# Rotating an 8192 x 8192 matrix: macro tiles of 2048 columns, with four load buffers of half the size and four store buffers

## Chip, cores and metric

One core of one Trainium2 chip. The metric is the device time of one launch in microseconds (us), the median of several runs. The kernel before takes 1275.95 us (three runs, 1274.87 to 1276.43).

## The reference

```python
x = np.random.randn(8192, 8192).astype(np.float32)   # 268.4 MB
np.rot90(x, 1)                                        # out[i, j] = x[j, 8191 - i]
```

Every element is read once and written once: 536.9 MB of traffic and no arithmetic.

## The kernel before

The matrix is handled in macro tiles of 1024 rows by 4096 columns. Loads bring 128 rows each (2 MB, 16 KB a row). VectorE copies each load into chunks of 128 x 512 with the order of columns reversed in each block of 128. TensorE transposes 128 x 128 blocks into PSUM, ScalarE copies PSUM into a store buffer, and ScalarE's queue issues a 2 MB store.

```python
R = 1024; RT = R // P; W = 4096; CH = 512; G = 4; PW = 2
...
    a_pool = ctx.enter_context(tc.tile_pool(name="a_pool", bufs=2))     # 2 x 16 KB a partition
    r_pool = ctx.enter_context(tc.tile_pool(name="r_pool", bufs=68))    # chunks, 2 KB each
    o_pool = ctx.enter_context(tc.tile_pool(name="o_pool", bufs=2))     # 2 x 16 KB
...
        for t0 in range(0, RT, q):
            if loads < 2:
                a = o_pool.tile([P, W], dt, tag="o")     # the first two loads borrow store buffers
            else:
                a = a_pool.tile([P, W], dt, tag="a")
            loads += 1
            ...                                          # nc.sync.dma_start(out=a, in_=x[...])
            ...                                          # VectorE: a -> chunks
        for g0 in range(0, C // P, G):
            ...                                          # 32 transposes, 2 ScalarE copies
            nc.scalar.dma_start(out=dst, in_=o[...])
```

A macro tile has 64 chunks, and a store tile needs chunks of all its eight loads. So the first store can go only when a whole macro tile is in. The last macro tile is cut into 2048, 1024 and 1024 columns. A function run at the end of the build, `whole_reads`, rewrites the read side of a transfer so that a row of a store buffer is read as one run of 16 KB, although it is written to HBM in four runs of 4 KB.

## Time and profile before

| what | value | from |
|---|---|---|
| span of the profiled run | 1274.2 us | page |
| PE, VectorE, ScalarE busy | 56%, 28%, 37% | page |
| DMA rate, 120 to 1100 us | 428 GB/s | table by stretches |
| load, store: issue to landing | 16.6 us, 15.9 us | page |
| median packet of 16 KB | 611 ns load, 615 ns store | packet records |

Engines at half load and DMA at 99% mean that only the DMA columns matter. One more view of the kernel before: VectorE's timeline from 20 to 50 us. Each line is the copy of one 2 MB load; the columns are start, busy time, and in brackets how long VectorE was idle before and for whom. (In such lines DVE is VectorE, ACT ScalarE, PE and PEld are TensorE's matmuls and weight loads, and L111 is a line of the kernel.)

```profile
22.76 2.77 DVE L111 COPY ar<-a 128x512 f32<-128x512 f32 x8 [2.12 <-DMA a<-in_x_dram]
29.79 2.77 DVE L111 COPY ar<-a 128x512 f32<-128x512 f32 x8 [4.25 <-DMA a<-in_x_dram]
35.39 2.77 DVE L111 COPY ar<-a 128x512 f32<-128x512 f32 x8 [2.83 <-DMA a<-in_x_dram]
42.46 2.77 DVE L111 COPY ar<-a 128x512 f32<-128x512 f32 x8 [4.29 <-DMA a<-in_x_dram]
```

The copies of the first four loads start 4.9 us apart, the fourth at 22.76 us. The next three come 5.6 to 7.1 us apart.

### The profile page before, as it was taken

The page shows a single profiled execution, that of the slowest core. Times are in us where ns is not written, and L with a number is a line of the kernel's source. Part 1 is how long each engine was busy: PE and PEld are TensorE (multiplying, and loading weights), DVE is VectorE, ACT ScalarE, POOL GpSimd, SP SyncE. Part 2 cuts the span into 40 slices and gives each one's busy share as a digit, 9 for nine tenths or more (in the row PEclk, how much of TensorE's full clock was granted, in tenths as well). Part 3 has the DMA queues.
Part 4 walks back from the last instruction along what each step waited for, and adds up shares of the span by engine and source line. Part 5 has one row for each costly group of instructions (what it writes and reads, how often), then busy time and mean ns, then how long its engine had stood idle before and what let it go on. Part 6 is the DMA issues. An engine that isn't in the chain of part 4 may idle for free.

```text
span 1274.2 us, 10388 instructions
## 1 busy us (share of the span) xinstructions
PE 719.2 (56%) x4096; PEld 685.5 (54%) x4096; DVE 355.2 (28%) x1024; ACT 466.9 (37%) x257; POOL 0.7 (0%) x6
## 2 busy tenths in 40 slices
PE   1455556556655665556546565565565665665564
PEld 0355556555554655556546555565555554665564
DVE  4422232223222322232223222322232222321210
ACT  0233343334334333343334333433343333434444
POOL 0000000000000000000000000000000000000000
PEclk9968686877777677776886867768777778678878
DMA  9999999999999999999999999999999999999998
GB/s 375 366 427 427 427 428 431 429 428 428 430 428 430 428 427 429 429 429 429 427 427 427 429 427 428 427 427 429 428 427 426 424 423 429 427 425 422 420 408 338
DMA packets 39105, 537.55 MB, mean 422 GB/s; under 512 B 4112, under 2 KB 4112, under 8 KB 6160
## 3 DMA queue, kind: packets, MB, share of 16 engines
q1 hardware_dynamic: 20480, 268.44, 49.8%
q10 hardware_dynamic: 18576, 268.44, 49.8%
q8 instruction: 32, 0.52, 0.2%
q14 instruction: 17, 0.14, 0.0%
HBM read 268.44 MB, written 268.44 MB: 421 GB/s over the span
## 4 chain that ended last, share of the span: by engine, by line
DMA 84%; DVE 12%; issue 2%; ACT 1%; PE 0%; DVEq 0%; SPq 0%; ACTq 0%
DMA a<-in_x_dram 81%; DVE ar L111 12%; DMA out_dram<-ot 3%; ACT ot L133 1%; PE ps L128 0%; DVEq L111 0%; SPq L100 0%; ACTq L133 0%; ACTq L141 0%
## 5 line engine op out<-in xcount | busy, mean ns | idle before, releaser
L128 PE MATMUL ps<-ident,ar 128*128 128x128 f32 x4096 | 719.2, 358 | 543.8 <-ACT ot L133 500.2
L128 PEld LDWEIGHTS ps<-ident,ar 128*128 128x128 f32 x4096 | 685.5, 192 | 577.3 <-ACT ot L133 530.5
L133 ACT COPY ot<-ps 128x2048 f32<-128x2048 f32 x256 | 465.6, 1870 | 789.3 <-DMA out_dram<-ot 733.5
L111 DVE COPY ar<-a 128x512 f32<-128x512 f32 x1024 | 355.2, 421 | 894.4 <-DMA a<-in_x_dram 894.4
L133 ACT ACT_TABLE_LOAD x1 | 1.3, 1283 | 10.9 <-DVE ar L111 10.9
masks.py:199 POOL TENSOR_SCALAR_AFFINE_SELECT ident<-ident 128x128 f32<-128x128 f32 x1 | 0.3, 292 | 0.1
masks.py:197 POOL MEMSET ident<- 128x128 f32 x1 | 0.2, 204 | 0.3 <-POOLq L160 0.3
L160 POOL MEMSET const-bfloat16-1.0<- 128x1 bf16 x1 | 0.1, 102 | 0.0
L160 POOL MEMSET const-uint8-127<- 128x1 uint8 x1 | 0.1, 102 | 0.0
L160 POOL MEMSET const-float32-0.0<- 128x1 f32 x1 | 0.1, 99 | 0.2 <-issue 0.2
L160 POOL MEMSET const-float32-1.0<- 128x1 f32 x1 | 0.1, 99 | 0.0
## 6 DMA issues: line engine op xcount, KB each, us to landing
a<-in_x_dram SPq DMA_DIRECT2D x128, 2048.0 KB, 16.6
out_dram<-ot ACTq DMA_DIRECT2D x127, 2048.0 KB, 15.9
out_dram<-ot ACTq DMA_DIRECT2D x2, 1024.0 KB, 5.7
```

The source lines that it names most:

```text
L111: nc.vector.tensor_copy(out=ar[:], in_=a[:, u, j * CH : (j + 1) * CH].rearrange("r (b m) -> r b m", m=P)[:, :, ::-1],)
L128: nc.tensor.transpose(ps[:, PW - 1 - w, t * P : (t + 1) * P], chunks[t, g * P // CH][:, g % (CH // P), :], ident,)
L133: nc.scalar.copy(o[:, G - PW - h : G - h, :], ps[:])
L160: nc = _bacc.Bacc("TRN2", target_bir_lowering=False, num_devices=1)
```

## The change

The intent: smaller macro tiles fill sooner, and four buffers on each side keep more transfers in flight. The sum of memory stays at about 200 KB a partition.

```diff
-W = 4096
+W = 2048
...
-        widths = [W] * (M // W)
+        widths = [2048] * 4
...
-            widths[-1:] = [2048, 1024, 1024]
+            widths = [2048, 2048, 2048, 1024, 1024]
...
-    a_pool = ctx.enter_context(tc.tile_pool(name="a_pool", bufs=2))
-    r_pool = ctx.enter_context(tc.tile_pool(name="r_pool", bufs=68))
-    o_pool = ctx.enter_context(tc.tile_pool(name="o_pool", bufs=2))
+    a_pool = ctx.enter_context(tc.tile_pool(name="a_pool", bufs=4))
+    r_pool = ctx.enter_context(tc.tile_pool(name="r_pool", bufs=52))
+    o_pool = ctx.enter_context(tc.tile_pool(name="o_pool", bufs=4))
...
-            if loads < 2:
-                a = o_pool.tile([P, W], dt, tag="o")
+            if loads < 4:
+                a = o_pool.tile([P, G * R], dt, tag="o")
```

Load rows become 8 KB and loads 1 MB; stores stay 2 MB with 16 KB read runs.

## The prediction

> **What bounds the kernel now.** I read the page's busy table and slices first, then the longest waits, then the DMA view and the table by stretches for the steady part, and last the timeline of the start. On the page:
>
> ```profile
> PE 719.2 (56%) x4096; PEld 685.5 (54%) x4096; DVE 355.2 (28%) x1024; ACT 466.9 (37%) x257; POOL 0.7 (0%) x6
> DMA  9999999999999999999999999999999999999998
> GB/s 375 366 427 427 427 428 431 429 428 428 430 428 430 428 427 429 429 429 429 427 427 427 429 427 428 427 427 429 428 427 426 424 423 429 427 425 422 420 408 338
> q1 hardware_dynamic: 20480, 268.44, 49.8%
> q10 hardware_dynamic: 18576, 268.44, 49.8%
> ```
>
> No compute engine is busy over 56%. The 16 DMA engines are: queue 1 (loads) and queue 10 (stores) together take 99.6% of their time, and the rate is flat at 427 to 430 GB/s except in the first two slices and the last two or three. Each queue moves 268.44 MB, which the problem fixes. 536.9 MB at 428.5 GB/s is 1253 us; the other 21 us of the 1274.2 us span lie in the two ends. The waits agree:
>
> ```profile
> DVE ar L111 <- DMA a<-in_x_dram: 894.4, 128, 15.4
> ACT ot L133 <- DMA out_dram<-ot: 733.5, 122, 11.4
> PEld ps L128 <- ACT ot L133: 530.5, 127, 11.5
> ```
>
> VectorE waits for loads, ScalarE for stores to free its buffer, TensorE for ScalarE: everybody waits for DMA in the end. Nowhere in the steady part does VectorE wait for TensorE. The DMA view from 120 to 1100 us:
>
> ```profile
> DMA packets 28797, 419.33 MB, mean 428 GB/s; under 512 B 3197, under 2 KB 3197, under 8 KB 3197
> q10 hardware_dynamic: 14379, 209.39, 50.4%
> q1 hardware_dynamic: 14379, 209.41, 50.1%
> ```
>
> Both queues carry equal packets there, and 100 loads and 100 stores in 980 us make one 2 MB load plus one 2 MB store every 9.8 us. Only the price of a byte on the DMA engines, and idle DMA at the ends, can move the time. By stretches (the last two columns are DMA busy share and GB/s):
>
> ```profile
> 4.00:20.00 16.00, 2.04 (x6) 0.87 (x6) 7.68 (x23) 1.28 (x1) 0.00 (x0) 1.00 1.00 430
> 20.00:50.00 30.00, 4.37 (x16) 2.78 (x17) 13.85 (x41) 0.00 (x0) 0.00 (x0) 1.00 0.92 349
> 50.00:80.00 30.00, 16.80 (x108) 15.65 (x106) 8.99 (x26) 11.04 (x7) 0.00 (x0) 0.77 1.00 412
> 120.00:1100.00 980.00, 572.89 (x3200) 549.16 (x3200) 277.50 (x800) 362.73 (x200) 0.00 (x0) 0.75 1.01 428
> 1140.00:1187.00 47.00, 29.08 (x192) 27.53 (x192) 11.10 (x32) 21.82 (x12) 0.00 (x0) 0.82 1.01 423
> 1240.00:1274.00 34.00, 16.59 (x128) 15.52 (x128) 2.77 (x8) 16.62 (x10) 0.00 (x0) 0.82 0.83 347
> ```
>
> From 20 to 50 us the rate falls to 349. The timeline tells why: four loads go out at the start (two into store buffers, two into load buffers); the fifth needs a load buffer and is issued only at 20.67 us, after the third has landed and VectorE has spent 2.77 us copying it out. From then on two load buffers alternate, loads land about every 6.3 us instead of every 4.9, and no store can go before 54 us.
>
> **What the Trainium skill says.** "DMA: Bandwidth & Descriptors", section "Where 436 GB/s comes from", puts the ceiling of the 16 engines at 435 GB/s. The trace agrees: 428 to 430. So no layout of buffers can gain much over the steady part. The same page, "Why small descriptors are slow (HBM only)", gives a fixed overhead per packet. The packet records of this trace agree in form: the median packet of 4096, 8192 and 16384 bytes took 159, 309 and 611 ns, a straight line with 8 to 9 ns fixed. (8 KB and 4 KB packets occur in the last tiles, which the kernel before already narrows.) The same page, "Queues, rings and completion order", says that an engine takes turns between queues packet by packet; the equal counts above agree. After the change a load packet is half a store packet, so while both queues hold work stores should get two thirds of the bytes. "SBUF — State Buffer", "The DMA setup-cost knee", charges about 2 us fixed to each transfer and so favours large ones; the 430 GB/s with four loads in flight shows that this is hidden when several overlap, so I charge nothing for 1 MB loads.
>
> **The change, part by part.** Compute is the same: 4096 transposes, 1024 VectorE copies of 421 ns, 256 ScalarE copies of 1870 ns, 129 stores. Loads are 256 of 1 MB instead of 128 of 2 MB, and their rows 8 KB instead of 16 KB.
>
> 1. Load packets. In the kernel before, 120 loads x 128 rows = 15360 packets are of 16 KB. Each becomes two of 309 ns, 618 against 611: +7 ns. 15360 x 7 / 16 engines = **+6.7 us**, all on the path, as DMA never rests.
> 2. Completion packets. Each DMA leaves one 4-byte packet of 9 ns on each engine. 128 more DMAs: **+1.2 us**. SyncE's issue of 0.33 us each is hidden.
> 3. Start. The first eight loads have buffers (four store, four load) and make a whole macro tile, so they run without any wait. Then a load buffer is away for VectorE's 4 x 0.35 = 1.4 us, the issue and some 2 us of start, while three other loads need 3 x 2.45 us: no gap. What the stretches lose now: 30 x (1 - 349/428) = 5.5 us, and 30 x (1 - 412/428) = 1.1 us. I give back **-6 us** of these 6.6. The 2 us to the first byte stays. That the first store goes at some 30 us instead of 54 is worth nothing by itself: bytes are bytes.
> 4. End. From 1240 us DMA is 0.83 busy, 34 x 0.17 = 6 us lost. Four store buffers should remove the waits for a store there (4 to 5 us before a ScalarE copy), but the last macro tile is the same 1024 columns: after its last load, copies, 64 transposes and the last store must follow. With store packets favoured 2:1 or 4:1 over loads, the store backlog will be gone by then, so this chain stands more exposed: I estimate 1.4 + some 7 + 4.9 + 5 us and two latencies, about 20 us, with 9.8 us of data. **+2 us**, uncertain by 4.
> 5. Bursts. Now load and store march 1:1 and both queues always hold two transfers. Afterwards four stores go at two thirds of the rate (7.3 us each, 29 us), then the store queue empties until the next macro tile is complete, some 10 us. DMA still has loads to do: 52 chunk buffers hold one macro tile (32) plus five loads, and four load buffers more. But switches cost something: in 1140 to 1187 us, where 8 KB loads meet 16 KB stores and the store queue runs dry, the rate is 423 against 428, 1.2% less. Load packets (40% of the bytes) explain half of it; the other half went with single packets of 500 to 1000 ns where a queue restarts. At 0.3% of 1250 us: **+3 us**, perhaps 0 and perhaps 12.
>
> Sum: +6.7 + 1.2 - 6 + 2 + 3 = +7 us; 1276 + 7 = 1283, and I say 1282.
>
> **Rivals.** (a) Deeper buffers win: if the lockstep of two transfers per queue were hiding a loss, four would show it. Against it: busy share 1.01 and 428 of 435 GB/s from 120 to 1100 us; at most the 12 us lost at the ends could come back, 1264. (b) The bursts make TensorE the bound: a store tile needs 32 transposes, 5.1 to 6.4 us in the timeline, so stores cannot be fed faster than about 2.1 MB / 5.8 us = 360 GB/s; that matters only if loads stop meanwhile, that is if chunk buffers run out. With 20 spare chunks against 4 before, I think not; if it did happen each macro tile could lose a microsecond or two, 32 to 64 us, 1310 to 1340. (c) The half-size rows read worse from HBM than the medians say, as the 423 stretch might mean if all its loss were the packets': then 1.5% on the whole, about 1295. (d) The restart losses vanish because the other queue is deep: 1277 to 1279.
>
> **Range and chances.** (d) and the sum with modest bursts make the middle, 1277 to 1288; (c) is the upper end; a perfect end and start the lower. 1270 to 1296 should hold it 8 times in 10. Within 2% is 1250 to 1301: gains have no room to reach 1250, as the steady part alone takes 1253; only (b), or (c) with bursts, passes 1301.
>
> **What would show it.** Queue 1 should have 37888 packets (31744 of 8 KB, 2048 of 4 KB, 4096 completions) and queue 10 the same 18576. The second slice should rise from 366 to 420 or more; the middle should read 422 to 427 instead of 428, with uneven slices; the 8 KB packet should have a median of 309 ns. Load time to landing should swing between about 10 us and 20 us where it is now a constant 16.6. VectorE's waits should still be for loads and ScalarE's more for TensorE than for stores. I am wrong if VectorE waits for TensorE in the middle (chunks), if the DMA share there falls under 0.98, or if the mean 8 KB packet exceeds 320 ns.

## The result and the profile after

1285.72 us (median of four runs, 1282.6 to 1289.65) against 1276.11 us: ratio 1.0079, 95% interval 1.005 to 1.0107. A ratio is the mean time of one kernel's runs over that of the other's in the same rounds, so it is not quite the ratio of the medians. The interval is clear of 1: it is a little slower, by about 10 us.

The page of the changed kernel, the lines that answer to those of before:

```profile
PE 611.6 (48%) x4096; PEld 572.9 (45%) x4096; DVE 366.8 (29%) x1024; ACT 467.8 (36%) x257; POOL 0.7 (0%) x6
GB/s 393 424 425 427 424 428 427 425 429 427 423 423 425 424 419 419 419 419 428 424 423 414 427 427 424 414 423 423 423 416 419 425 420 408 426 424 422 405 423 307
q1 hardware_dynamic: 37888, 268.45, 50.2%
q10 hardware_dynamic: 18576, 268.44, 49.6%
```

The second slice rose from 366 to 424: the start is repaired. The middle fell from a flat 428 to an uneven 408 to 429. The loads' queue holds exactly the 37888 packets foreseen. Its time is 50.2% of 1284.2 us, some 645 us, where it was 49.8% of 1274.2, some 635; the packet records say 645.2 against 634.9, and 636.9 against 634.5 for stores.

The waits, longest first (total us, times, longest):

```profile
DVE ar L111 <- DMA a<-in_x_dram: 860.5, 244, 10.5
PEld ps L128 <- ACT ot L133: 636.7, 128, 11.3
...
ACT ot L133 <- DMA a<-in_x_dram: 602.7, 80, 11.2
ACT ot L133 <- PE ps L128: 165.9, 48, 19.9
...
ACT ot L133 <- DMA out_dram<-ot: 10.3, 2, 5.4
```

ScalarE hardly waits for stores any more (733.5 us before, 10.3 now). But it waits for *loads*, 602.7 us. No copy of ScalarE reads a load buffer, so this needs an explanation; the timeline gives it (ACTq is the issue of a store by ScalarE's queue):

```profile
304.87 1.86 ACT L133 COPY ot<-ps 128x2048 f32<-128x2048 f32 x1
...
316.10 0.55 ACTq L141 DMA_DIRECT2D out_dram<-ot  x1
316.15 1.43 DVE L111 COPY ar<-a 128x512 f32<-128x512 f32 x4 [4.73 <-DMA a<-in_x_dram]
```

The store tile is complete at 306.73 us and its store is issued at 316.10, in the same moment as VectorE starts on a fresh load. The trace has eight completion semaphores for all DMAs, and the build hands them out in turn. The issue times read as if a DMA has to wait until the last one on its semaphore has landed. In the kernel before loads and stores alternate, and eight back in turn is always one of the same kind, which landed 23 us or more earlier. In the changed kernel there are two loads to a store, and eight back from a store in that turn is a load (five back in the order of issue). The records show it: of 98 stores issued from 120 to 1100 us, 97 were issued within 0.3 us of the landing of the load that last had their semaphore. So stores in flight averaged 1.27 and were never more than two. Counting from ScalarE's first copy into a store buffer to the landing, at most three of the four buffers were held at once, three of them for 25% of that time.

By stretches (after the window and its length, busy us and number of instructions of PE, PEld, VectorE, ScalarE and GpSimd, then TensorE's granted clock; the last two columns are DMA busy share and GB/s):

```profile
4.00:20.00 16.00, 4.09 (x12) 1.73 (x12) 8.59 (x24) 1.28 (x1) 0.00 (x0) 1.00 1.01 426
20.00:50.00 30.00, 18.55 (x122) 16.25 (x122) 11.45 (x32) 14.65 (x8) 0.00 (x0) 0.88 1.01 420
50.00:80.00 30.00, 17.48 (x122) 16.20 (x122) 8.60 (x24) 11.02 (x6) 0.00 (x0) 0.72 1.01 425
120.00:1100.00 980.00, 469.39 (x3151) 444.11 (x3152) 282.26 (x788) 359.07 (x198) 0.00 (x0) 0.75 1.01 422
1240.00:1284.00 44.00, 20.21 (x147) 18.11 (x145) 4.30 (x12) 18.38 (x10) 0.00 (x0) 0.77 0.81 341
```

From 20 to 50 us 420 GB/s instead of 349; in the middle 422 instead of 428, with DMA fully busy. So in the middle it is the packets that take longer, not idle engines. The medians are as before (309 ns for 8 KB, 614 for stores). Two measures from the packet records serve below, both for 120 to 1100 us:

- *Slow packets*: what packets took beyond the median of their size and queue, summed and divided by the 16 engines. It was 3.5 us before and is 11.5 us now.
- *Dry*: a queue is dry while fewer than two of the 16 engines work on it. The store queue was dry 0.5% of the time before and is dry 21% now.

Of the 11.5 us, 10.0 come from packets that start while neither queue is dry, and they gather about the restarts of the store queue (52 of them after more than 0.5 us dry). Of the 6.2 us of load packets, 2.3 fall in the first 2 us after a restart, with 6% of the packets; of the 5.3 us of store packets, 4.8 fall 2 to 6 us after one.

### The profile page after: what moved, and what is told of

The parts are those of the page before. It is cut to its first block, busy times and chain, and to the rows that moved or that the text cites. A ratio compares the mean times of both kernels' runs of the same rounds, so it can differ in the third digit from the quotient of the medians.

```text
span 1284.2 us, 10957 instructions
## 1 busy us (share of the span) xinstructions
PE 611.6 (48%) x4096; PEld 572.9 (45%) x4096; DVE 366.8 (29%) x1024; ACT 467.8 (36%) x257; POOL 0.7 (0%) x6
## 3 DMA queue, kind: packets, MB, share of 16 engines
q1 hardware_dynamic: 37888, 268.45, 50.2%
## 4 chain that ended last, share of the span: by engine, by line
DMA 89%; DVE 6%; PE 1%; issue 1%; ACT 1%; DVEq 0%; SPq 0%; ACTq 0%
DMA a<-in_x_dram 89%; DVE ar L111 6%; PE ps L128 1%; ACT ot L133 1%; DVEq L111 0%; SPq L100 0%; ACTq L141 0%; DVEq L174 0%; ACTq L133 0%
## 5 line engine op out<-in xcount | busy, mean ns | idle before, releaser
L128 PE MATMUL ps<-ident,ar 128*128 128x128 f32 x4096 | 611.6, 320 | 661.9 <-ACT ot L133 605.8
L128 PEld LDWEIGHTS ps<-ident,ar 128*128 128x128 f32 x4096 | 572.9, 168 | 700.4 <-ACT ot L133 636.7
L133 ACT COPY ot<-ps 128x2048 f32<-128x2048 f32 x256 | 466.5, 1870 | 800.9 <-DMA a<-in_x_dram 602.7
L111 DVE COPY ar<-a 128x512 f32<-128x512 f32 x1024 | 366.8, 421 | 898.7 <-DMA a<-in_x_dram 860.5
```

The costliest lines, as they stand in the source:

```text
L111: nc.vector.tensor_copy(out=ar[:], in_=a[:, u, j * CH : (j + 1) * CH].rearrange("r (b m) -> r b m", m=P)[:, :, ::-1],)
L128: nc.tensor.transpose(ps[:, PW - 1 - w, t * P : (t + 1) * P], chunks[t, g * P // CH][:, g % (CH // P), :], ident,)
L133: nc.scalar.copy(o[:, G - PW - h : G - h, :], ps[:])
```

## The experiments

Three theories. **P**: the price of more packets is the whole loss. **A**: engines take turns between the queues packet by packet, so 16 KB store packets beside 8 KB load packets drain the store queue faster than loads can refill it, and running dry and restarting costs. **T**: the semaphore shared with a load starves the store queue.

### Load packets of 8 KB in the kernel before (e1_half_rows)

```diff
-        for t0 in range(0, RT, q):
+        Cs = min(C, 2048); q = W // Cs
+        for t0, c in [(t, s) for t in range(0, RT, q) for s in range(0, C, Cs)]:
...              # in_=x[r0 + t0*P : r0 + (t0+q)*P, c0 + c : c0 + c + Cs]
```

> The kernel before with one thing changed: each 2 MB load takes two row blocks of 2048 columns instead of one of 4096, so its packets are 8 KB; macro tiles, number of DMAs and buffers stay (at most four transfers in flight). Theory P (the price of a packet: 2 x 309 - 611 = 7 ns on each of 15360): +6.7 us, about 1283, few slow packets in the middle. Theory A (unequal packets alone let the store queue run dry and restart, which costs slow packets): like the changed kernel in the middle, about 422 to 424 GB/s, 1287 to 1292. If the tie of completion semaphores is needed for the slow packets, there are none here, as P says.

Measured: 1321.38 us, ratio 1.0347 (1.0331 to 1.0363). P is far off, and even A's own number was too small. The DMA view from 120 to 1100 us, one rate per fortieth:

```profile
GB/s 363 427 425 396 405 427 427 375 428 427 379 429 426 399 405 427 426 372 426 427 374 427 426 396 408 426 426 368 427 422 354 432 423 395 408 426 426 381 430 428
```

It swings between full rate and 354 to 408. The store queue is dry 26% of the time, and the slow packets (23.7 us) sit mostly where loads run alone: 22 us of them start while the store queue is dry, and DMA is only 0.94 busy then. There two load buffers are in the same need as at the start, when 349 GB/s was reached. Stores finish early, then wait for the next macro tile, and loads alone with two buffers don't fill DMA. So this run adds the shortage of load buffers to the effect of unequal packets; the changed kernel, with four, has less of it. No store here follows closely on a load that had its semaphore, so T has no part in it.

### The same, with store packets of 8 KB too (e8_equal_8k)

```diff
-                    ap = [ap[0], [1, 1], [1, ap[1][1] * ap[2][1]]]
+                    ap = [ap[0], [2048, ap[1][1] * ap[2][1] // 2048], [1, 2048]]
```

> The run with half rows (8 KB load packets, 1321 us) with one more thing changed: the stores' reads are cut in two as well, so store packets are 8 KB too; nothing else. Packets are equal again, at 8 KB. Theory A (unequal packets drain the store queue): although every transfer now has smaller packets, it gets much faster, back to the kernel before plus the price of the packets, (7 ns x 15360 + 3 ns x 16384) / 16 = 10 us: 1284 to 1288, store queue dry under 3%. If small load packets themselves were slow with 2 MB loads, it stays at 1315 or above.

Measured: 1282.32 us, ratio 1.0042 (1.0029 to 1.0055). The same view:

```profile
GB/s 427 427 426 428 427 427 427 427 427 427 427 427 427 427 428 427 426 427 426 427 424 426 427 425 427 426 425 428 424 427 427 424 425 427 427 424 416 423 425 425
```

Making the stores' packets *smaller* wins 39 us and makes them equal; the store queue is dry 3.7% of the time. (Loads of 16 KB with stores of 8 KB were not run: that equal packets are better, and not just store packets no larger than the loads', is tried in this direction alone.) This run is also the price of small packets by itself, all other things as in the kernel before: +0.42%, 5.4 us for both directions, where the medians had said 10. In the records the packets of the two queues took 11.0 us more (1280.4 against 1269.4), while the span grew by 6.0: packet times overlap a little (busy share 1.01), and a sum of them is not time on the clock.

### The changed kernel with equal packets, in two ways

**Stores of 8 KB reads (e11_equal_reads)**, the same edit of `whole_reads`, nothing else.

> The changed kernel with the stores' reads cut in two, so that store packets are 8 KB as the load packets are; still 2 MB stores, four buffers, and every store still shares its completion semaphore with an earlier load. Theory A (unequal packets): store queue no longer dry, slow packets of some 9 us go, 3 us more for packets: 1278 to 1281. Theory T (the semaphore shared with a load starves the store queue): dry about 20% as it is, 1286 to 1290.

Measured: 1278.01 us, ratio 1.0009 (0.9997 to 1.0022). Its middle stretch, to be compared with the 422 GB/s of the changed kernel:

```profile
120.00:1100.00 980.00, 565.43 (x3168) 541.85 (x3168) 283.32 (x791) 358.91 (x199) 0.00 (x0) 0.75 1.01 425
```

Of 99 store issues from 120 to 1100 us, 98 still follow within 0.3 us on the landing of a load, as T wants it, but the store queue is dry 4% instead of 21% and the slow packets halve (5.7 us). At the end, DMA stands idle for 5.7 of the last 44 us, as in the kernel before (5.7; 8.2 in the changed kernel). T by itself starves nothing; the unequal packets carry the loss. Whether they would cost as much with four load buffers and no tie was not tested.

**Store tiles of half the size (e2_small_stores)**

```diff
-G = 4
+G = 2
-    ... name="o_pool", bufs=4
+    ... name="o_pool", bufs=8
```

> The changed kernel with store tiles of 8 KB (two blocks instead of four, eight buffers), so load and store packets are equal again, both 8 KB. Theory P: store packets double, 2 x 312 - 615 = 9 ns on 16384 at most, +9 us and 128 more completions +1.2: 1293 to 1297. Theory A (unequal packets make the store queue run dry): the store queue is almost never dry, the slow packets of some 8 us go, which pays for most of the packets: 1284 to 1289, dry share of the store queue under 5% where it is 21% now.

Measured: 1279.63 us, ratio 1.002 (1.0009 to 1.0032); better than A's range. Loads and stores alternate one to one here, so a store follows a store on its semaphore: up to four 1 MB stores are in flight, dry share 0.3%, slow packets 2.2 us. On the whole that is no better than e11 with its tie to loads, so removing the tie gains nothing in sum once packets are equal. By stretches it is less plain: the middle reads 426 GB/s against 425, but 1190 to 1240 us reads 372 against 407, and there are 128 more completions to pay for.

### Two store buffers (e3_two_stores)

```diff
-    ... name="o_pool", bufs=4
+    ... name="o_pool", bufs=2
-            if loads < 4:
+            if loads < 2:
```

> The changed kernel with two store buffers instead of four (first two loads in store buffers, not four): at most six transfers in flight, fewer than the eight completion semaphores. Theory T (stores wait for the load that last used their semaphore, which starves the store queue): stores wait for stores or TensorE again, the store queue is dry less than 21% of the time, slow packets about halve: 1280 to 1283. Theory A (unequal packets do it): dry share and time as they are, 1284 to 1288. If four store buffers were of real use, it gets slower, over 1289.

Measured: 1283.25 us, ratio 1.0052 (1.0037 to 1.0068); the interval overlaps that of the changed kernel. The premise of this test was wrong: I had thought that six transfers in flight would free the semaphores. They are handed out in turn whatever is free, and 98 of 99 stores still followed within 0.3 us on a load. Dry share 22%, slow packets 10.4 us: as in the changed kernel. What it does show is that taking away the third and fourth store buffer loses nothing.

### A spacer between the DMAs (e6_no_tie)

```diff
+            if loads % 2 == 0:
+                one = d_pool.tile([1, 1], dt, tag="one")
+                nc.sync.dma_start(out=one, in_=x[r0 : r0 + 1, c0 : c0 + 1])
```

> The changed kernel with one 4-byte load more after every second load, which no one reads; completion semaphores are handed out in turn, and with four transfers a round instead of three each store follows a store on its semaphore, not a load. Packets stay unequal. Theory T: slow packets halve, 1279 to 1282. Theory A: with unequal packets the store queue still runs dry about a fifth of the time, 1283 to 1289; stores in flight rise above the 1.27 of now only in bursts.

Measured: 1329.25 us, ratio 1.0417. A failed instrument. The spacers did not stay in their places: they gathered, and on SyncE's queue they stood behind loads that waited. From 120 to 1100 us 77 of 94 stores still shared their semaphore with a load and 16 with a spacer. From 150 to 330 us stores then waited for spacers:

```profile
ACT ot L138 <- DMA one<-in_x_dram: 132.3, 14, 9.9
```

It says nothing on A or T. The rate was 310 to 330 GB/s where stores waited for spacers.

### Two load buffers (e7_two_loads)

```diff
-    ... name="a_pool", bufs=4
+    ... name="a_pool", bufs=2
```

> The changed kernel with two 8 KB load buffers instead of four. If the four load buffers are what keeps DMA full while the store queue is dry, two of 1 MB cannot (a buffer is away 1.4 us for the copy, 0.4 for the issue and some 2 for the start, against 2.45 us for the other load): the load-only stretches fall to about 350 GB/s and the time goes to 1310 to 1330 as with half rows. If load buffers don't matter, 1284 to 1288.

Measured: 1396.47 us, ratio 1.0936. The direction is right, the size is not. Two things come together. Already with loads alone, 4 to 20 us, it reaches less than the 426 of four buffers:

```profile
4.00:20.00 16.00, 4.10 (x12) 1.73 (x12) 8.60 (x24) 1.28 (x1) 0.00 (x0) 1.00 0.94 387
```

And the load to which a store is tied is now the one issued just two before it (91 of 91), so a store starts when the loads end and the two take turns: both queues are dry over 40% of the time. With four load buffers the tie is five back, and e11 shows it harmless. So the change needs its four load buffers; how the 111 us against the changed kernel divide between the two effects stays open. The records say where the time went: DMA was still 0.99 busy from 120 to 1100 us, but store packets took 64.5 us beyond their median, 48.6 of them while the load queue was dry. Neither effect says why.

### Mending the start of the kernel before

The changed kernel showed that the start can be mended. Can the kernel before have that without small packets?

**First macro tile in narrow tiles (e5_start)**: `widths[:1] = [1024, 1024, 2048]`.

> The kernel before with the first 4096-column macro tile split into 1024, 1024 and 2048 columns (2 MB loads as before): the first tile is complete after two loads, so stores start near 17 us and fill the DMA while two load buffers alternate. If the loss at the start (349 GB/s from 20 to 50 us) is what the changed kernel won back, this wins it without small packets: 1270 to 1272, ratio 0.995 to 0.997. If not, 1276.

Measured: 1278.98 us, ratio 1.0017 (1.0003 to 1.0031). The stretch from 20 to 50 us rises to 404 GB/s, but narrow tiles have small load packets beside 16 KB stores, 50 to 80 us reads 399, and 2.6 us of slow packets follow from 120 to 169 us (0.1 before).

**First macro tile in two of half height (e9_half_height)**, so packets stay 16 KB:

```diff
+            if r0 == 0 and c0 == 0:
+                yield 0, 0, C, R // 2
+                yield R // 2, 0, C, R // 2
...              # G, PW and the store's rows follow from the height
```

> The kernel before with its first macro tile cut in height instead of width: twice 512 rows of 4096 columns, so load packets stay 16 KB and equal to the store packets. Complete after four loads, which all have buffers, so stores start near 30 us instead of 54 and fill the DMA while the two load buffers alternate. If unequal packets are what took back the gain of the start made of narrow tiles (1279), this one keeps it: 1272 to 1274. If an early start of stores is worth nothing, 1276 to 1277.

Measured: 1276.92 us, ratio 0.9998 (0.9986 to 1.0011). From 20 to 50 us 399 GB/s, but 80 to 120 us now reads 405 (431 before) and 120 to 200 us 415 (429). The stores of the small tiles are done before the first full macro tile has come in, and the stretch of loads alone comes then. It was moved, not removed.

**And the last store tiles in load buffers (e10_both_ends)**

> The same, and the last macro tile puts its two store tiles in the load buffers, which are free by then, so they do not wait for the stores before: 2 us more, 1270 to 1272. If the end is set by TensorE and not by store buffers, no change.

Measured: 1275.75 us, ratio 0.9998 (0.9986 to 1.0011): no change. ScalarE's waits for stores in the last 30 us fell from 8.7 us (e9) to 4.6 and nothing came of it, so the buffers of the last two store tiles do not set the end.

**All cuts in height (e12_all_heights)**: 256, 256, 512 rows first, 512, 256, 256 last, no narrow tile.

> No narrow tiles at all: the first macro tile is cut in height to 256, 256, 512 rows, the last to 512, 256, 256, all of 4096 columns, so every load packet and store packet is 16 KB to the end; the last stores in load buffers as before. The stretch from 1140 to 1240 us, 423 and 411 GB/s in the kernel before with 8 KB and 4 KB load packets, should read 427: 2.5 us. With the start: 1267 to 1270. Against it: stores of 256 rows write runs of 1 KB; if those are slow, 1272 or more.

Measured: 1285.98 us, ratio 1.0074 (1.006 to 1.0087). From 1140 to 1187 us it reads 428 as hoped (423 before), but 50 to 80 us falls to 356 and 1190 to 1240 to 394: tiles of 256 rows, whose stores write runs of 1 KB, give back more. Whether it is the short runs or the order of the small tiles was not separated.

**Four buffers for the first eight loads (e13_four_at_start)**: store buffers are idle until the first store, so loads 5 and 6 may borrow them too.

```diff
-            if loads < 2:
+            if loads < 8 and loads % 4 < 2:
```

> The kernel before with one line changed: loads 5 and 6 also go into the two store buffers, which are idle until the first store near 48 us, so all of the first eight loads have four buffers between them. The first macro tile has to be loaded before stores can march; cutting it smaller only moved that stretch to later (1277). If the stretch with two buffers (349 GB/s) is the loss, eight loads take 4.9 us each: the first tile is complete near 43 us instead of 48, 20 to 50 us reads 410 or more, middle unchanged at 428: 1270 to 1272, ratio 0.995 to 0.997. If the loss turns up elsewhere again, 1276.

Measured: 1272.02 us (1271.09 to 1273.74) against 1276.4; ratio 0.9967 (0.9953 to 0.998). Correct, and the fastest of all. Its VectorE timeline, to be held against the one of before:

```profile
22.71 2.78 DVE L111 COPY ar<-a 128x512 f32<-128x512 f32 x8 [2.11 <-DMA a<-in_x_dram]
27.61 2.77 DVE L111 COPY ar<-a 128x512 f32<-128x512 f32 x8 [2.13 <-DMA a<-in_x_dram]
32.50 2.77 DVE L111 COPY ar<-a 128x512 f32<-128x512 f32 x8 [2.11 <-DMA a<-in_x_dram]
38.03 2.77 DVE L111 COPY ar<-a 128x512 f32<-128x512 f32 x8 [2.75 <-DMA a<-in_x_dram]
42.87 2.78 DVE L111 COPY ar<-a 128x512 f32<-128x512 f32 x8 [2.07 <-DMA a<-in_x_dram]
```

Loads now come 4.8 to 5.5 us apart; the eighth is copied at 42.87 us, 5.0 us sooner than before, and the gain of 4.2 us (0.33% of 1276.4) is kept to the end because the middle stays at 428 GB/s.

## Why the prediction was right, and where its terms were not

The time was foreseen as 1282 in a range of 1270 to 1296; it is 1285.72. The view of what bounds the kernel and the sign of the net effect held. The size, 10 us where 6 to 7 were foreseen, came out so near partly by luck, as two errors have opposite signs. By its steps:

1. **Load packets, +6.7 us.** The median of 309 ns and the count were exact. The price was overstated: e8 measured 5.4 us for loads *and* stores, where the medians gave 10. In the proportion of its two terms (6.7 to 3.1) the loads' part is some 3.7 us, an estimate.
2. **Completions, +1.2 us.** Not tested by itself.
3. **Start, -6 us.** Right in mechanism: 20 to 50 us went from 349 to 420 GB/s. e13 makes the same repair alone and wins 4.2 us. In the changed kernel it is some 5.4 us, an estimate worked out from e11: 5.4 for packets in both directions plus 1.2 for completions, less the start, is the 1.2 us (0.09%) by which e11 is slower. Whatever else e11 does differently is in that figure.
4. **End, +2 us.** From 1240 us on the loss is 44 x 0.19 = 8.4 us against 5.8: +2.6. The waits for stores did go (ScalarE has none from 1200 us on, 26.1 us before), but nothing came of it; e10 agrees for the last two store tiles.
5. **Bursts, +3 us.** This is the term that was mis-sized. That unequal packets empty the store queue was the right mechanism, but the pattern was wrong and the size nearly three times too small. Stores do not go in bursts of four: shared semaphores let at most two be in flight, and loads land a steady 16.8 to 19.9 us after issue, not 10 to 20 in swings. The store queue ran dry 21% of the time. Making packets equal (e11) won 0.70%, 8.9 us (5 to 13 by the two intervals; 7.6 between the two profiled runs), although its store packets cost some 1.7 us more, an estimate from the 5.4: the unequal packets cost about 10.6 us. The end's 2.6 are in it, since e11's end is as before; that leaves 8.0 for the middle against the 3 foreseen. Its own figures would have given more than 3: a loss of 1.2% of which the packets are 40% of 7/611, or 0.5%, leaves 0.7% of 1250, some 9 us. It took 0.3% without saying why.

Sum of what was found: +3.7 + 1.2 - 5.4 + 10.6 = +10.1, against 0.79% of 1276.1 = 10.1. It closes by construction, as step 3 and the last term both lean on e11; e8 and e13 are the independent checks. The luck is that step 1 was some 3 us too large and step 5 some 5 us too small.

Of the rivals, (a), deeper buffers win, is out: with four loads and four stores in flight and equal packets (e2) the middle reads 426 GB/s, not more than the 428 of before. (b), TensorE as the bound, did not come. But the sign that was named for being wrong there did show: VectorE waited for TensorE in the middle, 30.2 us in 9 waits, so the 52 chunks do run out at times. It cost nothing that can be seen: DMA stayed at 1.01, and e2 runs at 1279.63 us with 204.9 us of such waits. (c), half-size rows that read worse, is out: e11 keeps them and is 0.09% slower than the kernel before. (d), no loss from restarts, did not come with unequal packets; with equal ones e11 (1278.01) lies in its 1277 to 1279 and e2 close by. What the 423 GB/s stretch loses stays undivided: e8, with equal packets, reads 424 there. Two of the signs were wrong: ScalarE waits for loads far more than for TensorE (602.7 us against 165.9), and the loads' time to landing does not swing.

Open: why packets are slow. In the changed kernel they gather about the restarts of the store queue, in e1 where loads run alone with two buffers, in e7 where stores run alone. That dryness itself makes them slow is not shown: where loads run alone in the changed kernel, slow packets add 0.8 us in 207.

## What to carry to other kernels

When a kernel is bound by DMA with loads and stores at once, try equal read runs in the two directions before large ones: here 8 KB with 8 KB cost 0.4% and 8 KB with 16 KB cost 3.5% with two load buffers, 0.1% and 0.8% with four and a better start. Before adding buffers, check in the trace which DMA a store's issue really follows, and look for buffers that are idle in the phase that is short of them: lending the two store buffers to two loads more won 4.2 us, where the whole change lost 10.

## What the Trainium skill lacked or had wrong

- "DMA: Bandwidth & Descriptors", section "Queues, rings and completion order", says that engines take turns by packets. It does not say what follows when packets differ: while neither queue was dry in the changed kernel, 14653 load packets of 8 KB started beside 11947 store packets of 16 KB, 1.2 to one, so stores had 1.6 times the bytes; with equal packets (e11) it was 23738 to 23800. Between e1 and e8, with two load buffers, this was worth 39 us of 1321. Nor does it say which side sets the size of a packet. Here it is the read side: stores that write runs of 4 KB stand in the records as packets of 16 KB, and of 8 KB once their reads are cut in two (e8).
- "SBUF — State Buffer", section "The DMA setup-cost knee", gives 1 MiB transfers about 340 GB/s. With four buffers for them loads alone ran at 426 GB/s, with two (e7) at 387 from 4 to 20 us, its four borrowed buffers included. With enough of them in flight the fixed part that the page's fit charges to every transfer does not show.
- On no page: completion semaphores handed out in turn to loads and stores tie a store's issue to a load. 97 of 98 store issues of the changed kernel came within 0.3 us of such a landing.
